# Experts of a two-layer mixture: quarter-row gathers, 32x32 block transposes, and another spread of the products over the quadrants

## The chip, the cores and the metric

One core of a Trainium2 chip runs the whole program. The metric is the device time of one execution in microseconds (us). Short names of the engines: PE is TensorE's matmul side and PEld its weight loads, DVE is VectorE, ACT is ScalarE, POOL is GpSimd and SP is SyncE, which issues most of the DMAs.

## What is computed

The reference is two blocks of two layers each, in float32. The part that matters here is the feed-forward part of the second block, in both of its layers: a hierarchical mixture of experts. Each token (768 of them in the first such layer, 512 in the second) picks two of 32 experts and is sent through both:

```python
def expert_block(args):
    xb, e = args
    return (jax.nn.silu(xb @ w1[e]) * (xb @ w3[e])) @ w2[e]
...
y = yb.reshape(n_rows, d)[dest] * sw[:, None].astype(h.dtype)
return jnp.zeros_like(h).at[stok].add(y)
```

A token has 1024 features, an expert 512 inner ones; w1 and w3 are 1024 x 512, w2 is 512 x 1024. So an expert has 6.29 MB of weights. Two picks of 768 tokens over 32 experts are 48 rows for an expert on average, two of 512 are 32.

## The kernel before, in words

The layers run one after the other: `rwkv`, `mla`, `ab`, the first mixture `m0`, `c`, the second mixture `m1`. Only the two mixtures are touched. `moe` (L2889) lets the router finish (`route`, L2701), then runs `experts` (L2918), then `overflow` (L3056) for what does not fit in the static slots.

**The slots.** Each expert has 96 slots. `route` works out, for slot s of expert e, the token in it: `rd[s, e]` (L2786 to L2789), by one-hot products on PE (L2785), a copy on ACT (L2788) and an addition on DVE (L2789). An empty slot points to a row of zeros on reading and past the end on writing, where the write is dropped.

**One expert, as `experts` has it.** `gather` (L2936) is one indirect DMA issued by POOL: 96 rows of 4 KB from `hbuf` in DRAM to `xg` [96, 1024], with two buffers. `turn` (L2942) makes `xT` [128, 8, 96] of it: eight transposes on PE (L2947), a copy on DVE (L2951) and one on ACT (L2949). The first products take each block of 32 slots as weights (128 x 32, one column quadrant of PE) and stream 512 columns of w1 or w3:

```python
for a in range(3):
    mm(H1[q(a)], lhsT=xT[:, kb, q(a)], rhs=w[0][:, kb, :], **f)
mm(H1[q(3)], lhsT=xT[:, kb, q(2)], rhs=w[1][:, kb, :], **f)
for a in range(2):
    mm(H3[q(a)], lhsT=xT[:, kb, q(a)], rhs=w[1][:, kb, :], **f)
```

(L3021 to L3025.) So of the six products of each of eight `kb`, quadrants 0 and 1 have two each, quadrants 2 and 3 one each. `act` (L2954) makes u of them: tanh on ACT (L2957), three operations on DVE (L2958 to L2960). `uturn` (L2963) transposes u on PE (L2966), with a copy on ACT (L2968). The second products are `yab` (L3008 to L3011: 16 products, eight each in quadrants 2 and 3) and `yc` (L3013 to L3015: eight products, four each in quadrants 0 and 1). `gate` (L2971) makes weight times gate, on ACT (L2974, L2977) and POOL (L2978, in the first mixture only). `yput` (L2981) multiplies by it on DVE (L2985, L2986), and POOL issues an indirect DMA (L2987) that adds the rows to `acc` (`out` in the second mixture) in DRAM.

**The loop.** Step e (L2999) has the first products of expert e and the second products of expert e - 1, mixed. The order of the instructions within the engines is not that of the code: a scheduler with a simulated time line sets it, except inside `manual_schedule`, where the engines named keep the order of the code. Before the change, `experts` has none.

**The weights.** They come in thirds of 2 MB (w1, w3, w2 of one expert) to seven places in turn (`load`, L1498, the DMA on L1503), nearly all issued by SP. A third is issued when the place's earlier content has been used: w3 of expert e takes the place of w1 of expert e - 2, w2 of e that of w3 of e - 2, w1 of e that of w2 of e - 3.

**The start.** The router's last products for the overflow (`pto`, L2883) and for the slots' weights (L2849) come in steps 1 and 0 of the loop, when the generator `own.way` is sent on.

Of the kernel before, what the change touches and what calls it, by code (L numbers as in the profile page):

```python
# [16 lines left out]
P = 128  # L17
# [14 lines left out]
# ---------------------------------------------------------------- host layout  # L32
# [11 lines left out]
def const_arrays(np):  # L44
    """Masks, identities and rope tables: they depend on shapes alone."""
# [43 lines left out]
    put("tid", np.arange(6)[None, :] * P + i[:, None])  # L89
    off["base"] = (base, 0)  # L90
# [28 lines left out]
    # by pairs of heads: queries (64 plain features, 32 to rotate, those with their halves swapped), keys, values, gate  # L119
# [12 lines left out]
    # by units: a key, its four queries, its value  # L132
# [18 lines left out]
# ---------------------------------------------------------------- program  # L151
# [4 lines left out]
def rsqrt(g, v, n, name, pool=None):  # L156
    """v [128, n] -> v ** -0.5, by Newton steps from the exponent's half."""
# [36 lines left out]
def stats(g, tiles, name, junk):  # L194
    """rsqrt(mean(t * t) + eps) of each [128, 1024] tile: [128, n]."""
# [9 lines left out]
def hT_make(g, psum, pool, tiles, A, B, put, name):  # L205
    """tiles: token tiles of one stream; (x rstd) transposed, times A[:, fb] plus B[:, fb], into put(fb)."""
# [16 lines left out]
def affine(g, pool, gcol, MC, sc0, sh0, v, name):  # L223
    """norm gain times (1 + scale), and shift, as [128, 8] columns."""
# [8 lines left out]
def row_bcast(g, psum, MC, g0, v, dst, tag="mm"):  # L233
    """Column block MC[:, g0 : g0 + 8, v] as a row on every partition: dst [128, 1024]."""
# [10 lines left out]
def setup(g):  # L245
# [12 lines left out]
    # silu of the four conditioning vectors, one column of 32 each  # L258
# [10 lines left out]
def rwkv_layer(g):  # L269
# [8 lines left out]
    with contextlib.ExitStack() as own, tc.tile_pool(name="rwB", bufs=1) as keep:  # L278
        # tanh(xw @ w1) and xa @ a1, feature-major; the former with a row of ones for w0
# [62 lines left out]
def rwkv_lerp(g, s, j, affine=False):  # L342
    """The j-th interpolation of the rows; those that are projected by blocks also go to DRAM, by token tiles."""
# [5 lines left out]
    for fb in range(9):  # L349
# [9 lines left out]
        for (A, B, hB), o, n in zip(s.affine, (1, 259), (256, 512)) if affine and fb < 8 else ():  # L359
            # the first and the last row of a stream have one neighbour only  # L360
# [8 lines left out]
def rwkv_first(g, s, L, wap, dst):  # L369
    """Products of a lerp with 128 columns; yields between them."""  # L370
# [21 lines left out]
def mm(g, out, **kw):  # L392
    """A product; how much of the array it keeps busy goes into g.act, and its time in ns into g.ns."""
# [9 lines left out]
def apart(g, later, *earlier):  # L403
    """Accesses to different quadrants of a PSUM bank: no order between them."""
# [4 lines left out]
class Stream:  # L409
    """Parts of work in order; each part is due some time after the one before it, or what that one yields."""  # L410
# [18 lines left out]
class Mix:  # L429
    """Puts streams into one order for the array: what is due and has got the least far. In between, the large  # L430
# [2487 lines left out]
def experts(g, l, own, rd, wi):  # L2918
# [5 lines left out]
    with tc.tile_pool(name="exT", bufs=2, reuse_waits="tile") as pt, \  # L2924
# [74 lines left out]
        for e in range(NE + 1):  # L2999
# [18 lines left out]
            for kb in range(8):  # L3018
# [7 lines left out]
                if e and kb == 1:  # L3026
                    uT = uturn(u)
# [213 lines left out]
```

## Time and profile before

| What | us |
|---|---|
| median of 3 runs | 4262.28 |
| lowest and highest of them | 4259.32, 4266.27 |
| the profiled execution: its span, first to last instruction | 4260.4 |
| PE busy in it | 3810.4 |
| DVE, ACT, POOL busy in it | 2104.5, 1334.9, 735.4 |

The profile is one execution of the program. The page gives no other time of that execution than its span, 1.9 us below the median of the runs; what lies around the span is not shown. A float32 product of 512 columns shows as two records on PE, each with a weight load of its own. "x8" is a count of records, "mean ns" the mean duration of one, and what follows "<-" is what ended an engine's idle time. DMA shares are of the core's 16 DMA engines.

### The profile page before, as it was taken

The page shows a single profiled execution, that of the slowest core. Times are in us where ns is not written, and L with a number is a line of the kernel's source. Part 1 is how long each engine was busy: PE and PEld are TensorE (multiplying, and loading weights), DVE is VectorE, ACT ScalarE, POOL GpSimd, SP SyncE. Part 2 cuts the span into 40 slices and gives each one's busy share as a digit, 9 for nine tenths or more (in the row PEclk, how much of TensorE's full clock was granted, in tenths as well). Part 3 has the DMA queues.
Part 4 walks back from the last instruction along what each step waited for, and adds up shares of the span by engine and source line. Part 5 has one row for each costly group of instructions (what it writes and reads, how often), then busy time and mean ns, then how long its engine had stood idle before and what let it go on. Part 6 is the DMA issues. An engine that isn't in the chain of part 4 may idle for free. (4 is left out here: it accounts for less than half of the span.)

```text
span 4260.4 us, 85407 instructions
## 1 busy us (share of the span) xinstructions
PE 3810.4 (89%) x35570; PEld 2419.0 (57%) x35570; DVE 2104.5 (49%) x5178; ACT 1334.9 (31%) x3262; POOL 735.4 (17%) x668
## 2 busy tenths in 40 slices
PE   6798999999868899987998799999788996999998
PEld 4677777777754667656765333333378863333332
DVE  7435545455543566568765422222376754222222
ACT  3244334434422354333442112112245531111111
POOL 1111001101100111122112222222233312111110
PEclk9899999999977999988999899999889998999999
DMA  6755566666672110210111689899511126888885
GB/s 225 211 173 175 173 185 200 186 201 206 187 209 58 65 55 29 70 41 23 44 51 71 228 323 348 341 346 349 205 40 49 40 69 243 318 334 341 344 336 191
DMA packets 396625, 775.21 MB, mean 182 GB/s; under 512 B 60172, under 2 KB 312012, under 8 KB 370636
## 3 DMA queue, kind: packets, MB, share of 16 engines
q1 hardware_dynamic: 372024, 704.56, 47.1%
q0 software_dynamic: 17504, 56.66, 4.6%
q10 hardware_dynamic: 6708, 8.49, 0.6%
q8 instruction: 282, 4.62, 0.4%
q14 instruction: 107, 0.88, 0.1%
HBM read 711.90 MB, written 66.62 MB: 183 GB/s over the span
## 5 line engine op out<-in xcount | busy, mean ns | idle before, releaser
L3022 PE MATMUL H<-wex,xT 128*32 128x512 f32 x3072 | 772.7, 600 | 0.1
L3025 PE MATMUL H<-wex,xT 128*32 128x512 f32 x2048 | 546.2, 593 | 0.0
L3011 PE MATMUL Y<-wex,uT 128*32 128x512 f32 x2048 | 534.9, 594 | 1.8 <-ACTq L3064 1.8
L3023 PE MATMUL H<-wex,xT 128*32 128x512 f32 x1024 | 521.0, 603 | 0.0
L2951 DVE COPY xT<-pxT 128x384 f32<-128x384 f32 x64 | 35.7, 558 | 598.4 <-PE pxT L2947 595.9
L3025 PEld LDWEIGHTS H<-wex,xT 128*32 128x32 f32 x2048 | 124.2, 110 | 301.8 <-issue 301.5
L3022 PEld LDWEIGHTS H<-wex,xT 128*32 128x32 f32 x3072 | 160.2, 109 | 232.9 <-issue 221.0
L400 PE MATMUL pd<-dw,dl 128*128 128x128 f32 x1536 | 241.7, 301 | 34.1 <-DMA dl<-Ld 25.0
L3015 PE MATMUL Y<-wex,uT 128*32 128x512 f32 x1024 | 236.8, 593 | 0.0
L400 PEld LDWEIGHTS pd<-dw,dl 128*128 128x128 f32 x1536 | 203.2, 204 | 53.2 <-DMA dl<-Ld 25.4
L400 PE MATMUL pd<-dl,dw 128*128 128x128 f32 x1344 | 218.5, 300 | 8.4 <-ACT rk L521 4.6
L1202 ACT ACTIVATE prob<-S,smx 128x768 f32<-128x768 f32 (+3 forms) x160 | 125.7, 786 | 238.2 <-DVE smx L1197 214.0
L2974 ACT ACTIVATE R<-R,wi 96x1024 f32<-96x1024 f32 x64 | 73.4, 1148 | 395.4 <-DVE yo L2986 391.9
L400 PEld LDWEIGHTS pd<-dl,dw 128*128 128x128 f32 x1344 | 178.5, 201 | 27.6 <-issue 10.6
L2485 PE MATMUL pu<-wc,hT 128*128 128x384 f32 (+1 forms) x768 | 184.1, 328 | 1.0 <-ACT hT L1350 1.0
L1140 DVE COPY RT<-ZU 32x128 f32<-32x128 f32 x192 | 54.4, 284 | 255.3 <-PE ZU L400 225.3
L2949 ACT COPY xT<-pxT 128x384 f32<-128x384 f32 x64 | 30.7, 479 | 444.9 <-PE pxT L2947 444.9
L2958 DVE SCALAR_TENSOR_TENSOR th<-th,H 96x512 f32<-96x512 f32 x64 | 43.7, 683 | 244.0 <-ACT th L2957 244.0
L1195 DVE TENSOR_REDUCE smx<-S 128x1 f32<-128x768 f32 (+3 forms) x160 | 128.6, 804 | 67.6 <-PE S L1873 37.7
L3011 PEld LDWEIGHTS Y<-wex,uT 128*32 128x32 f32 x2048 | 132.7, 110 | 49.2 <-issue 46.9
L3015 PEld LDWEIGHTS Y<-wex,uT 128*32 128x32 f32 x1024 | 60.5, 110 | 148.3 <-issue 148.3
L1226 PE MATMUL ppT<-cst,prob 128*128 128x128 f32 x784 | 121.7, 287 | 24.7 <-DVE prob L2291 14.6
(594 smaller groups left out, 8345.7 us busy)
## 6 DMA issues: line engine op xcount, KB each, us to landing
wex<-in_w SPq DMA_DIRECT2D x186, 2048.0 KB, 12.6
dl<-Ld SPq DMA_DIRECT2D x180, 512.0 KB, 3.9
wmod<-in_mod_w SPq DMA_DIRECT2D x128, 512.0 KB, 5.2
dw<-in_rw_in SPq DMA_DIRECT2D x30, 512.0 KB, 5.5
wex<-in_w POOLq DMA_DIRECT2D x6, 2048.0 KB, 9.8
wcr<-in_c_in SPq DMA_DIRECT2D x28, 384.0 KB, 4.0
Ld<-lerp SPq DMA_DIRECT2D x18, 512.0 KB, 6.5
lerp<-in_mod_w SPq DMA_DIRECT2D x4, 2048.0 KB
```

What stands on the lines that cost most here:

```text
L400: return g.nc.tensor.matmul(out, **kw)
L1140: ev = f(dst, Up[u])
L1195: nc.vector.tensor_reduce(m[:, 0:1], S[:, :n], mybir.AxisListType.X, ALU.max)
L1202: nc.scalar.activation(p[:, :n], S[:, :n], AF.Exp, scale=scale, bias=m[:, 1:2], accum_out=m[:, 2:3])
L1226: nc.tensor.transpose(pp[:, k, :], p[:, (i + k) * P:(i + k + 1) * P], g.C("ident"))
L2485: nc.tensor.matmul(o, lhsT=x, rhs=w[:, a:3, kb, :], start=kb == i == 0, stop=kb == 7 and i == 2)
L2974: nc.scalar.activation(G_, Gb[0][0:S], AF.Copy, scale=wi[:, 0, e:e + 1])
L3011: mm(Y[h][q(2 + a)], lhsT=uT[:, fb, q(a)], rhs=w2[:, fb, 512 * h:512 * h + 512], start=fb == 0, stop=fb == 3)
L3015: mm(Y[h][q(h)], lhsT=uT[:, fb, q(2)], rhs=w2[:, fb, 512 * h:512 * h + 512], start=fb == 0, stop=fb == 3)
L3022: mm(H1[q(a)], lhsT=xT[:, kb, q(a)], rhs=w[0][:, kb, :], **f)
L3023: mm(H1[q(3)], lhsT=xT[:, kb, q(2)], rhs=w[1][:, kb, :], **f)
L3025: mm(H3[q(a)], lhsT=xT[:, kb, q(a)], rhs=w[1][:, kb, :], **f)
```

## The change

`gather` becomes three indirect DMAs. The DRAM rows are seen as quarter rows of 256 features, and DMA a brings block a of 32 slots to all 128 partitions: partition 32 q + j gets quarter q of slot j. `route` works out the indices of the quarter rows, `rq` [128, 3, 32]. `turn` is one instruction on DVE that transposes 32x32 blocks, straight to `xT` [128, 3, 8, 32] in SBUF. The quadrants of the products depend on the expert's parity (`hb`, 0 or 2), the second products of the last block of slots (`c`) are split in two halves, one at the end of the step and one in the first two `kb` of the next, and they have a PSUM tile of their own (`Yc`). `experts` runs with PE in the order of the code. `th` and the operations on L2957 and L2958 have 128 partitions instead of 96. The comments and docstrings that the change also drops are left out of the diff here.

```diff
@@ const_arrays
     put("tid", np.arange(6)[None, :] * P + i[:, None])
+    put("row4", i // 32)
@@ route
+    first4 = sc([1], "first4")
+    V.tensor_scalar(first4, g.C("row4"), 4.0 * ntk, None, ALU.add)
+    quad = sc([3, 4, 32], "quad", BF16)
+    V.tensor_copy(quad, g.C("ident")[:, 0:SLOTS].rearrange("p (a j) -> p a j", a=3).unsqueeze(2).to_broadcast([P, 3, 4, 32]))
...
         nc.tensor.matmul(pt_[0:SLOTS], lhsT=oh[:, i], rhs=vv[:, i], start=i == 0, stop=i == K - 1)
+    two = sc([2, 32], "two", BF16)
+    V.tensor_copy(two[0:SLOTS], pt_[0:SLOTS])
+    rq = own.rq = keep.tile([P, 3, 32], U32, name="rq")
+    pq = ps.tile([P, 3, 2, 32], F32, name="pq", tag="aux")
+    for a in range(3):
+        nc.tensor.matmul(pq[:, a], lhsT=quad[0:SLOTS, a].rearrange("p g j -> p (g j)"), rhs=two[0:SLOTS], start=True, stop=True)
+    part4 = sc([3, 32], "part4")
+    nc.scalar.activation(part4, pq[:, :, 1], AF.Identity, scale=4.0, bias=first4)
+    V.scalar_tensor_tensor(rq, pq[:, :, 0], 4.0, part4, ALU.mult, ALU.add)
@@ moe
-        experts(g, l, into, rd, wi)
+        with tc.manual_schedule(engines=PEO):
+            experts(g, l, into, rd, wi)
@@ experts
+    quarters = hbuf[:, :].rearrange("n (q f) -> (n q) f", q=4)
...
-            tc.tile_pool(name="psX", bufs=2, space=PSUM) as psx:
+            tc.tile_pool(name="psX", bufs=1, space=PSUM) as psx:
...
         def gather(e):
-            xg = pt.tile([S, D], F32, name="xg", tag="xg")
-            own.gather = nc.gpsimd.indirect_dma_start(out=xg, out_offset=None, in_=hbuf[:, :],
-                                         in_offset=bass.IndirectOffsetOnAxis(ap=rd[:, e:e + 1], axis=0))
+            xg = pt.tile([P, 3, 256], F32, name="xg", tag="xg")
+            for a in range(3):
+                own.gather = nc.gpsimd.indirect_dma_start(out=xg[:, a], out_offset=None, in_=quarters,
+                                                          in_offset=bass.IndirectOffsetOnAxis(ap=own.rq[:, a, e:e + 1], axis=0))
             return xg

         def turn(xg):
-            xT = pt.tile([P, 8, S], F32, name="xT", tag="xT")
-            for h in range(2):
-                p = psx.tile([P, 4, S], F32, name="pxT", tag="tr")
-                for k in range(4):
-                    nc.tensor.transpose(p[:, k, :], xg[:, 4 * h + k::8], ident[0:S, 0:S])
-                if h:
-                    nc.scalar.copy(xT[:, 4:8, :], p)
-                else:
-                    nc.vector.tensor_copy(xT[:, 0:4, :], p)
+            xT = pt.tile([P, 3, 8, 32], F32, name="xT", tag="xT")
+            nc.vector.transpose(xT.rearrange("p a k t -> p (a k) t"), xg.rearrange("p a (i k) -> p a k i", k=8))
             return xT
...
+        class Second:
+            def __init__(self, e, u, w2, hb):
+                self.e, self.u, self.w2, self.hb, self.lb = e, u, w2, hb, 2 - hb
+                self.i = 0
+            def start(self):
+                self.uT = uturn(self.u)
+                self.Y = [psy.tile([P, 512], F32, name="Y%d" % h, tag="Y%d" % h) for h in range(2)]
+            def ab(self):
+                h, fb = self.i // 4, self.i % 4
+                self.i += 1
+                for a in range(2):
+                    mm(self.Y[h][q(self.lb + a)], lhsT=self.uT[:, fb, q(a)], rhs=self.w2[:, fb, 512 * h:512 * h + 512], start=fb == 0, stop=fb == 3)
+            def c(self, fb):
+                if fb == 0:
+                    self.Yc = psy.tile([P, 512], F32, name="Yc", tag="Yc")
+                for h in range(2):
+                    mm(self.Yc[q(self.hb + h)], lhsT=self.uT[:, fb, q(2)], rhs=self.w2[:, fb, 512 * h:512 * h + 512], start=fb == 0, stop=fb == 3)
...
             for kb in range(8):
                 if cur:
                     f = dict(start=kb == 0, stop=kb == 7)
-                    for a in range(3):
-                        mm(H1[q(a)], lhsT=xT[:, kb, q(a)], rhs=w[0][:, kb, :], **f)
-                    mm(H1[q(3)], lhsT=xT[:, kb, q(2)], rhs=w[1][:, kb, :], **f)
+                    for a, to in ((0, hb), (1, hb + 1), (2, lb)):
+                        mm(H1[q(to)], lhsT=xT[:, a, kb, :], rhs=w[0][:, kb, :], **f)
+                    mm(H1[q(lb + 1)], lhsT=xT[:, 2, kb, :], rhs=w[1][:, kb, :], **f)
                     for a in range(2):
-                        mm(H3[q(a)], lhsT=xT[:, kb, q(a)], rhs=w[1][:, kb, :], **f)
-                if e and kb == 1:
-                    uT = uturn(u)
-                if e and kb >= 2:
-                    yab(i)
-                    i += 1
+                        mm(H3[q(hb + a)], lhsT=xT[:, a, kb, :], rhs=w[1][:, kb, :], **f)
+                if old and kb < 2:
+                    old.c(2 + kb)
+                    if kb == 1:
+                        old.put_c()
+                if y and kb == 1:
+                    y.start()
+                if y and kb >= 2:
+                    y.ab()
                 if kb == 5 and e + 1 < NE:
                     xTn = turn(xg)
...
-            if e:
-                G_ = gate(e - 1)
-            if e:
-                for k in range(4):
-                    if i < 8:
-                        yab(i)
-                        i += 1
-                    yc(k)
-                yput(Y, e - 1)
+            if y:
+                for k in range(2):
+                    y.ab()
+                    y.c(k)
+                y.put_ab()
+            old = y
             if cur:
-                prev = (act(H1, H3), w[2])
+                y = Second(e, act(H1, H3, hb), w[2], 2 - hb)
...
+        for k in (2, 3):
+            old.c(k)
+        old.put_c()
```

Here `hb = 2 * (e % 2)` and `lb = 2 - hb` are set at the top of a step. `put_ab` and `put_c` are the two halves of the former `yput`: the first two blocks of slots, with `gate`, and the last block with the adding DMA.

## Rows read from the trace of the kernel before

**Rows 1.** Page, part 1: busy us (share), records of each engine.

```profile
PE 3810.4 (89%) x35570; PEld 2419.0 (57%) x35570; DVE 2104.5 (49%) x5178; ACT 1334.9 (31%) x3262; POOL 735.4 (17%) x668
```

**Rows 2.** A stretch of 21 us: length, busy (PE, PEld, DVE, ACT, POOL), clock, DMA share, GB/s.

```profile
2474.00:2495.00 21.00, 21.00 (x166) 7.37 (x160) 5.51 (x9) 3.85 (x5) 4.79 (x3) 1.00 0.95 365
```

**Rows 3.** PE in order of time over one step: start us, length us, instruction.

```profile
2717.12 0.72 PE L2966 MATMUL puT<-cst,u 96*128 96x96 f32 x4
2717.77 0.63 PE L3022 MATMUL H<-wex,xT 128*32 128x512 f32 x3
...
2725.68 1.13 PE L2947 MATMUL pxT<-cst,xg 96*128 96x96 f32 x8
...
2731.49 0.60 PE L3015 MATMUL Y<-wex,uT 128*32 128x512 f32 x2
...
2731.92 1.89 PE L3015 MATMUL Y<-wex,uT 128*32 128x512 f32 x8
...
2737.19 0.72 PE L2966 MATMUL puT<-cst,u 96*128 96x96 f32 x4
```

**Rows 4.** DMA queues over one step, 2717.8 to 2737.87 us.

```profile
DMA packets 658, 7.00 MB, mean 349 GB/s; under 512 B 108, under 2 KB 108, under 8 KB 272
```

**Rows 5.** DMA queues, 2692.5 to 2699.5 us: packets, MB, share of 16 engines.

```profile
q1 hardware_dynamic: 198, 2.98, 99.9%
```

**Rows 6.** DMA queues, 2861.5 to 2867.5 us, an adding DMA beside the weights.

```profile
q1 hardware_dynamic: 110, 1.69, 67.2%
q0 software_dynamic: 97, 0.38, 31.4%
```

**Rows 7.** DMA queues, 2728.5 to 2730 us, a gather with no weights under way.

```profile
q0 software_dynamic: 76, 0.31, 76.4%
```

**Rows 8.** DMA queues, 3250 to 3260 us, another stage: packets of 1 KB.

```profile
q1 hardware_dynamic: 1438, 1.42, 51.5%
```

**Rows 9.** DMA issues, whole span: count, median us to landing; adding DMAs of both mixtures.

```profile
acc<-yo,rd POOLq DMA_INDIRECT x32, 11.4
...
out<-yo,rd POOLq DMA_INDIRECT x32, 11.2
```

**Rows 10.** All engines, 2708.8 to 2709.9 us: end of an expert's w1, next issue.

```profile
2708.88 0.59 PE L3023 MATMUL H<-wex,xT 128*32 128x512 f32 x1
...
2709.52 0.33 SPq L1503 DMA_DIRECT2D wex<-in_w  x1
```

**Rows 11.** Groups by line, whole span: block transposes on DVE, POOL's work.

```profile
L2978 POOL TENSOR_TENSOR R<-R,R 96x1024 f32<-96x1024 f32 x32 | 90.3, 2823 | 8.5 <-ACT R L2977 8.5
...
L2938 POOL DMA_INDIRECT xg<-hbuf,rd x64 | 59.5, 930 | 477.6 <-PE pxT L2947 474.7 <-DVE nb L2823 1.6 <-DVE blk L2866 0.7
...
L1004 DVE STREAM_TRANSPOSE F<-AB 128x512 f32<-128x512 f32 x16 | 16.1, 1042 | 5.1 <-ACT AB L993 5.0
```

**Rows 12.** In order of time, start of the first mixture: turn, first product.

```profile
2402.77 1.54 PE L2947 MATMUL pxT<-cst,xg 96*128 96x96 f32 x8 [6.10 <-DMA xg<-hbuf,rd]
...
2406.09 1.07 PE L3022 MATMUL H<-wex,xT 128*32 128x512 f32 x3
```

**Rows 13.** PE in order of time: step 1's start and last `uturn` of each mixture.

```profile
2423.30 0.63 PE L3022 MATMUL H<-wex,xT 128*32 128x512 f32 x3
...
2443.71 0.87 PE L2883 MATMUL pto<-bv,oho 128*128 128x48 f32 x6
...
3053.43 0.72 PE L2966 MATMUL puT<-cst,u 96*128 96x96 f32 x4
...
3609.05 0.63 PE L3022 MATMUL H<-wex,xT 128*32 128x512 f32 x3
...
4235.78 0.72 PE L2966 MATMUL puT<-cst,u 96*128 96x96 f32 x4
```

**Rows 14.** DVE and ACT in order of time: `act` of one expert.

```profile
2709.57 0.59 ACT L2957 ACTIVATE th<-H 96x512 f32<-96x512 f32 x1 [2.29 <-PE H L3023]
...
2711.68 0.69 DVE L2960 SCALAR_TENSOR_TENSOR u<-th,H 32x512 f32<-32x512 f32 x1
```

More of the change, by code (lines that the diff above doesn't have):

```diff
@@ L2936, in gather, with act @@
         def gather(e):
-            xg = pt.tile([S, D], F32, name="xg", tag="xg")
-            own.gather = nc.gpsimd.indirect_dma_start(out=xg, out_offset=None, in_=hbuf[:, :],
-                                         in_offset=bass.IndirectOffsetOnAxis(ap=rd[:, e:e + 1], axis=0))
+            xg = pt.tile([P, 3, 256], F32, name="xg", tag="xg")
+            for a in range(3):
+                own.gather = nc.gpsimd.indirect_dma_start(out=xg[:, a], out_offset=None, in_=quarters,
+                                                          in_offset=bass.IndirectOffsetOnAxis(ap=own.rq[:, a, e:e + 1], axis=0))
             return xg
         def turn(xg):
-            xT = pt.tile([P, 8, S], F32, name="xT", tag="xT")
-            for h in range(2):
-                p = psx.tile([P, 4, S], F32, name="pxT", tag="tr")
-                for k in range(4):
-                    nc.tensor.transpose(p[:, k, :], xg[:, 4 * h + k::8], ident[0:S, 0:S])
-                if h:
-                    nc.scalar.copy(xT[:, 4:8, :], p)
-                else:
-                    nc.vector.tensor_copy(xT[:, 0:4, :], p)
-            return xT
-        def act(H1, H3):
-            th = new("th", [S, 512], 1)
+            xT = pt.tile([P, 3, 8, 32], F32, name="xT", tag="xT")
+            nc.vector.transpose(xT.rearrange("p a k t -> p (a k) t"), xg.rearrange("p a (i k) -> p a k i", k=8))
+            return xT
+        def act(H1, H3, hb):
+            lb = 2 - hb
+            th = new("th", [P, 512], 1)
             u = new("u", [S, 512])
-            nc.scalar.activation(th, H1[0:S], AF.Tanh, scale=0.5)
-            nc.vector.scalar_tensor_tensor(th, th, 1.0, H1[0:S], ALU.add, ALU.mult)
-            nc.vector.scalar_tensor_tensor(u[0:64], th[0:64], 0.5, H3[0:64], ALU.mult, ALU.mult)
-            nc.vector.scalar_tensor_tensor(u[64:96], th[64:96], 0.5, H1[96:128], ALU.mult, ALU.mult)
+            nc.scalar.activation(th, H1, AF.Tanh, scale=0.5)
+            nc.vector.scalar_tensor_tensor(th, th, 1.0, H1, ALU.add, ALU.mult)
+            nc.vector.scalar_tensor_tensor(u[0:64], th[q(hb, 2)], 0.5, H3[q(hb, 2)], ALU.mult, ALU.mult)
+            nc.vector.scalar_tensor_tensor(u[64:96], th[q(lb)], 0.5, H1[q(lb + 1)], ALU.mult, ALU.mult)
             return u
@@ L2979, in gate @@
             return G_
-        def yput(Y, e):
-            yo = new("yo", [S, D])
-            for h in range(2):
-                cs = slice(512 * h, 512 * h + 512)
-                nc.vector.tensor_tensor(out=yo[0:64, cs], in0=G_[0:64, cs], in1=Y[h][64:128], op=ALU.mult)
-                nc.vector.tensor_tensor(out=yo[64:96, cs], in0=G_[64:96, cs], in1=Y[h][32 * h:32 * h + 32], op=ALU.mult)
-            nc.gpsimd.indirect_dma_start(out=acc[:, :], out_offset=bass.IndirectOffsetOnAxis(ap=rd[:, e:e + 1], axis=0),
-                                         in_=yo, in_offset=None, bounds_check=own.nt * P - 1, oob_is_err=False, compute_op=ALU.add)
@@ L2990, in experts, with put_ab, put_c @@
-        mm = nc.tensor.matmul
+        mm = nc.tensor.matmul
+        class Second:
[15 more added lines that the diff above has]
+                    mm(self.Yc[q(self.hb + h)], lhsT=self.uT[:, fb, q(2)], rhs=self.w2[:, fb, 512 * h:512 * h + 512], start=fb == 0, stop=fb == 3)
+            def put_ab(self):
+                self.G = gate(self.e)
+                self.yo = new("yo", [S, D])
+                for h in range(2):
+                    cs = slice(512 * h, 512 * h + 512)
+                    nc.vector.tensor_tensor(out=self.yo[0:64, cs], in0=self.G[0:64, cs], in1=self.Y[h][q(self.lb, 2)], op=ALU.mult)
+            def put_c(self):
+                for h in range(2):
+                    cs = slice(512 * h, 512 * h + 512)
+                    nc.vector.tensor_tensor(out=self.yo[64:96, cs], in0=self.G[64:96, cs], in1=self.Yc[q(self.hb + h)], op=ALU.mult)
+                nc.gpsimd.indirect_dma_start(out=acc[:, :], out_offset=bass.IndirectOffsetOnAxis(ap=rd[:, self.e:self.e + 1], axis=0),
+                                             in_=self.yo, in_offset=None, bounds_check=own.nt * P - 1, oob_is_err=False, compute_op=ALU.add)
@@ L2997, in experts @@
         w = own.weights(0)
-        prev = None
+        y = old = None
         for e in range(NE + 1):
             cur = e < NE
+            hb = 2 * (e % 2)
+            lb = 2 - hb
             if cur:
@@ L3003, in experts @@
                 H3 = psh.tile([P, 512], F32, name="H3", tag="H3")
-            if e:
-                u, w2 = prev
-                Y = [psy.tile([P, 512], F32, name="Y%d" % h, tag="Y%d" % h) for h in range(2)]
-            def yab(i):
-                h, fb = i // 4, i % 4
-                for a in range(2):
-                    mm(Y[h][q(2 + a)], lhsT=uT[:, fb, q(a)], rhs=w2[:, fb, 512 * h:512 * h + 512], start=fb == 0, stop=fb == 3)
-            def yc(fb):
-                for h in range(2):
-                    mm(Y[h][q(h)], lhsT=uT[:, fb, q(2)], rhs=w2[:, fb, 512 * h:512 * h + 512], start=fb == 0, stop=fb == 3)
-            i = 0
             for kb in range(8):
```

3 lines of the change are left out of this document (1 added, 2 removed).

## The prediction

> **What bounds the kernel now.** The page comes first: PE is busy for 89% of the span, far ahead of DVE with 49% [rows 1]. Then stretches of 21 us through both mixtures: PE is busy for the whole stretch, at a granted clock of 1.00, while the DMA engines are busy for up to 0.95 of it [rows 2]. So PE sets the step of one expert, but the transfers are close behind it. Third, PE in order of time over one step [rows 3]: from `uturn` to `uturn` it takes 2737.19 - 2717.12 = 20.07 us. Inside, a round of records follows the last after 0.43 us (2731.49 to 2731.92), up to four quadrants in a round; a product is two records, so 0.86 us of its quadrant. Quadrants 0 and 1 have 16 + 4 = 20 products in a step, quadrants 2 and 3 have 16. The fullest quadrant therefore needs 20 x 0.86 = 17.2 us; `uturn` takes 0.65 (2717.12 to 2717.77) and `turn` 1.13. That is 19.0, and 1.1 us more go to rounds that are not full: the last row but one shows eight records of the last block, two quadrants at a time.
>
> **PE after the change.** By the code, the fuller pair of quadrants in a step has 16 first products and 2 of `c`, the other pair 8 first products, 8 of `ab` and 2 of the older `c`: 18 each, written in rounds of four. 18 x 0.86 = 15.5, plus 0.65 for `uturn`; `turn` is gone. I add 0.25 for emptying the array round `uturn`, between 0 and the 1.1 lost now: 16.4 us, between 16.15 and 17.25.
>
> **The transfers after it.** They then decide, so a step's DMA time has to be added up. Per step 7.00 MB move now [rows 4], 6.29 of them weights. Alone, the weights keep the engines 99.9% busy at 2.98 MB in 7 us, 426 GB/s [rows 5]: 14.8 us for an expert. The adding DMA: beside one of 0.38 MB, some 92 rows, the weights moved 1.69 MB in 6 us instead of 2.56 [rows 6], a loss of 0.87 MB or 2.0 us. Ordinary experts have 48 rows in the first mixture and 32 in the second, yet these DMAs land after 11.4 and 11.2 us [rows 9], so I take 2.0 for all: 96 slots over 16 engines are six to an engine, and the engine that has six full ones is as late with few rows as with many. By bytes it would be 0.2 MB, 0.5 us, the lower end. The Trainium skill (DMA: Bandwidth & Descriptors, Queues, rings and completion order) has each DMA engine take turns between its queues, a packet at a time; the two equal landings agree. By that rule a step comes to the sum below, by bytes alone to 1.5 us less.
>
> The gather now has 384 packets of 1 KB in place of 96 of 4 KB, the same bytes. The trace of before has no indirect packets of 1 KB. Plain ones took 0.515 x 16 x 10 us / 1438 = 57 ns each [rows 8]; indirect ones of 4 KB 0.764 x 16 x 1.5 us / 76 = 241 ns [rows 7]. I take 57, as a packet's time goes with its bytes in all these rows (16 KB of weights take 615 ns: 16 x 7 us over 2.98 MB / 16 KB): 384 x 57 / 16 engines = 1.4 us. By bytes at 426 GB/s it would be 0.9, at 241 ns it would be 5.8.
>
> Sum: 14.8 + 2.0 + 1.4 = 18.2 us a step, 1.8 above PE's 16.4. At the lower ends it is 16.2 and PE's 16.4 rules; at the upper it is 22.6. Can the queue be kept full? SP issues the third that takes w1's place 0.05 us after its last record (2708.88 + 0.59 = 2709.47, issue at 2709.52) [rows 10]. In the new order that issue stands some 2.6 us (three rounds of products) ahead of the next expert's start, so the next batch begins as the last of the earlier one lands. w1, whose place is now used until the second `kb` of the next step, 3.4 us in, is issued later than before, but w3 and w2 stand ahead of it on SP with 2 x 4.9 us to move; that costs nothing as long as they do.
>
> **Other engines.** DVE: a block transpose of 512 columns took 1042 ns [rows 11], so 768 take 1.56, in place of a copy of some 0.56; with 5.5 us busy in 21 now [rows 2] it has room, and xT is needed only two `kb` later. ACT loses a copy. POOL issues three gathers of 0.93 instead of one and has 2.82 for the gates in the first mixture [rows 11]: with the adding DMA about 7 us of 18. A gather may start when `turn` has freed its buffer, two steps before it is needed, so even a landing of 16 us (24 packets an engine, each behind one of weights at 615 + 57 ns) is covered. `act` ends 2712.37 - 2709.57 = 2.8 us after tanh starts [rows 14]; the new `uturn` comes 1.7 (tail) + 3.4 (two `kb`) = 5.1 us after the first products. Should DVE do `put_ab` first, PE could wait for about 0.6 us, hidden while the transfers leave it 1.8 idle.
>
> **Start and end of a mixture.** `route` gains a copy, three small products, and indices that pass ACT and DVE as before: 1.1 us by its neighbours, all ahead of the gather. The third gather is issued 2 x 0.93 = 1.9 later. `turn` before, from its first record to the first product, took 2406.09 - 2402.77 = 3.3 us [rows 12]; the block transpose with its wait some 1.8. Together +1.5 a mixture (0 to 4). Step 1 has `pto` of the overflow in PE's order: 6 records take 0.87 [rows 13], 24 take 3.5, and I allow 0.7 for waits on its one-hots (0 to 3): 15.5 + 0.65 + 4.2 = 20.35, say 20.5. The last expert's products run half empty as now, 10 rounds instead of about 9.3: +0.6.
>
> **Sum.** From step 1 to the last `uturn`, 31 steps, the mixtures now take 3053.43 - 2423.30 = 630.1 and 4235.78 - 3609.05 = 626.7 us [rows 13]. After: 20.5 + 30 x 18.2 = 566.5 each. Gains 63.6 + 60.2 = 123.8, less 2 x 1.5 and 2 x 0.6: 119.6. From the span of 4260.4 that gives 4140.8; the median of the runs stands 1.9 above that span, so 4143.
>
> **Rivals.**
> A: the transfers overlap better than I add them up, and PE's 16.4 rules. 60 steps x 1.8 less: 4035. For it: the lower ends. Against: 14.8 is weights alone at 99.9% busy.
> B: the chip gives no more over whole steps than it gives now. The best stretch of 21 us moved 365 GB/s [rows 2]; 7.00 MB at that rate are 19.2 us, 60 x 1.0 more: 4203. For it: no long stretch is above that. Against: the 426 of 7 us, and PE now leaves pauses between batches.
> The Trainium skill (DMA: Bandwidth & Descriptors, Where 436 GB/s comes from) puts the limit of HBM for a core at about 358 GB/s, which speaks against this change: 19.6 us a step by it. The 426 GB/s measured over 7 us do not agree.
> C, the slower one: the quarter rows cost by the packet. At 241 ns the gather takes 5.8 us of the engines, a step 22.6, 60 x 4.4 more than forecast: 4407. It decides from a step of 20.2, where the 119.6 are used up: (20.2 - 16.8) x 16 / 384 = 142 ns a packet. For it: the only indirect packets measured take 241. Against: their bytes.
> D: the even spread is not achieved, PE needs as many rounds as now and only `turn` is saved: 20.07 - 1.13 = 18.9 a step, 60 x 0.7 more: 4185. Against: the new order goes round the quadrants without a break.
>
> **How the numbers follow.** Forecast 0.56, A 0.10, B 0.16, C 0.09, D 0.09. The range leaves out A and C: 4080 (steps of 17.2, the adding DMA at half its price) to 4215 (19.4, a gather packet at 107 ns). Faster is all but C, 0.91; C may stop near its deciding point, so slower 0.07 and the same 0.02. Within 0.2%, 8.5 us, is about what a measurement of this kernel can't tell from no change.
>
> **What would show it.** Right: `uturn` to `uturn` at 17.8 to 18.6 us, PE waiting for `wex` before a step's first product, rounds of four without gaps, DMA share near 1.0. Wrong: steps of 16.4 without waits (A); DMA share near 1.0 with 1 KB packets far above 57 ns (C); DMA share well below 1.0 and PE waiting for u, xT or a late issue, a step on which I have put no price.

## The result, and the profile after

The kernel after takes 4142.12 us (median of 4 runs, 4135.81 to 4143.87), the kernel before in the same series 4262.54 (4259.32 to 4266.27). The ratio is 0.9711, with a 95% interval from 0.9697 to 0.9725: 2.9% faster. The profiled execution of after has a span of 4141.0 us, 119.4 less than that of before; forecast were 119.6. The number is close, but the way to it is not quite the one I wrote down.

Part 1 of the page of after, to be held against [rows 1]:

```profile
PE 3610.6 (87%) x35064; PEld 2310.0 (56%) x35064; DVE 2163.4 (52%) x5186; ACT 1305.2 (32%) x3200; POOL 863.5 (21%) x796
```

PE has 200 us less work, DVE and POOL have more. But only 119 us of the 200 came off the time: PE now waits. For what, the groups by line of the page say (busy, mean ns | idle before them, and what ended it):

```profile
L3056 PE MATMUL H<-wex,xT 128*32 128x512 f32 x3072 | 568.5, 612 | 68.0 <-DMA wex<-in_w 51.6
L3057 PE MATMUL H<-wex,xT 128*32 128x512 f32 x1024 | 542.6, 613 | 15.1 <-DMA wex<-in_w 15.1
...
L2958 POOL DMA_INDIRECT xg<-hbuf,rq x192 | 184.4, 960 | 531.8 <-DVE xT L2965 446.8
...
L2965 DVE STREAM_TRANSPOSE xT<-xg 128x768 f32<-128x768 f32 x64 | 102.3, 1598 | 83.1 <-PE H L3059 79.2
```

L3056 and L3057 are the first products with w1 and with w3. They waited 51.6 and 15.1 us for weights (`wex`). The block transpose takes 1.60 us (1.56 forecast), a gather's issue 0.96 (0.93).

Now the steps. PE in order of time in after, the `uturn` of five steps in a row, in the columns of [rows 3]:

```profile
2523.94 0.60 PE L2982 MATMUL puT<-cst,u 96*128 96x96 f32 x3
2540.17 0.60 PE L2982 MATMUL puT<-cst,u 96*128 96x96 f32 x3
2556.64 0.60 PE L2982 MATMUL puT<-cst,u 96*128 96x96 f32 x3
2582.50 0.60 PE L2982 MATMUL puT<-cst,u 96*128 96x96 f32 x3
2598.74 0.60 PE L2982 MATMUL puT<-cst,u 96*128 96x96 f32 x3
```

The steps are 16.23, 16.47, 25.86 and 16.24 us. So PE keeps its own pace of 16.24 us (16.4 forecast) in most steps, and every seventh step is 6.6 to 10 us longer; of the others some are longer by up to 5.4 us, in most sevens two. Read in this way through both mixtures, the mean of the 31 steps is 18.25 us in the first and 18.15 in the second, against the forecast 18.2. Step 1 (long, with `pto` in it) and the last step (short, 14.5 us) are in that mean. The long ones come every seven steps, in both mixtures at the same experts: 25.86, 26.29, 25.13, 22.86 in the first and 26.27, 25.73, 25.44, 24.04 in the second. Step 1 of each takes 24.6 and 25.1.

One long step from nearby, all engines in order of time, 2568 to 2578 us, with what ended the idle time in brackets:

```profile
2568.28 1.58 DVE L2965 STREAM_TRANSPOSE xT<-xg 128x768 f32<-128x768 f32 x1
...
2568.91 0.60 PE L3021 MATMUL Yc<-wex,uT 128*32 128x512 f32 x2
...
2576.99 1.07 PE L3056 MATMUL H<-wex,xT 128*32 128x512 f32 x3 [7.47 <-DMA wex<-in_w]
...
2577.85 1.07 PE L3056 MATMUL H<-wex,xT 128*32 128x512 f32 x3
```

xT has been there since 2569.86; the first product of expert 9 waits 7.47 us for its w1. Then its records take 1.07 us where they took 0.60: PE, after having stood still, works at the lower of its two clock levels (1.2 GHz) for some rounds: from 2577 to 2580 us the granted clock is 0.50, from 2583 us on it is 1.00 again. The view of three longer stretches (length, busy PE, PEld, DVE, ACT, POOL, granted clock, DMA share, GB/s) shows it, against [rows 2]:

```profile
2542.00:2556.00 14.00, 14.00 (x135) 4.96 (x128) 4.91 (x6) 2.63 (x3) 6.00 (x5) 1.00 1.02 415
2574.00:2598.00 24.00, 21.01 (x176) 6.47 (x180) 6.26 (x8) 3.37 (x4) 5.84 (x4) 0.86 0.79 301
2705.00:2725.00 20.00, 19.39 (x156) 5.90 (x160) 4.38 (x6) 3.37 (x4) 3.91 (x2) 0.86 0.82 298
```

In the undisturbed steps the transfers run at 415 GB/s with the engines fully busy. After a long wait the clock is 0.86 and the DMA share falls to 0.79: PE stood still and released no place, and SP issued nothing from 2567.83 to 2582.64 us. The DMA queues over 400 us, 2500 to 2900 (packets, MB, share of 16 engines), against [rows 4]:

```profile
DMA packets 14978, 150.31 MB, mean 376 GB/s; under 512 B 3408, under 2 KB 3408, under 8 KB 6600
...
q1 hardware_dynamic: 9393, 136.76, 84.0%
q0 software_dynamic: 5554, 13.09, 12.1%
```

q1 has the weights: 136.76 MB are 21.74 experts of 6.29 MB. The two queues were busy for 96.1% of 400 us, so 384.4 / 21.74 = 17.7 us of DMA time a step. The table below gives this figure for the other kernels, always from the same 400 us. In these 400 us the engines idle for the other 3.9%, 0.7 us a step.

Start and end, to be held against [rows 12] and [rows 13] (PE and DVE in order of time):

```profile
2409.04 1.55 DVE L2965 STREAM_TRANSPOSE xT<-xg 128x768 f32<-128x768 f32 x1 [1.05 <-DMA xg<-hbuf,rq]
...
2410.85 1.07 PE L3056 MATMUL H<-wex,xT 128*32 128x512 f32 x3 [8.33 <-DVE xT L2965]
...
2426.76 0.63 PE L3056 MATMUL H<-wex,xT 128*32 128x512 f32 x3
...
2996.12 0.73 PE L2982 MATMUL puT<-cst,u 96*128 96x96 f32 x4
...
3551.57 0.63 PE L3056 MATMUL H<-wex,xT 128*32 128x512 f32 x3
...
4117.83 0.72 PE L2982 MATMUL puT<-cst,u 96*128 96x96 f32 x4
```

From step 1 to the last `uturn` the mixtures take 569.4 and 566.3 us (forecast 566.5 each); 60.8 and 60.5 us are gained there, and 1.8 of these 121.2 are lost at the starts and ends (4.2 forecast).

**Which load is late.** The trace names all thirds `wex`. The compiled program has them in SP's order, here for the experts 8 to 11 (an expert's three tiles have neighbouring numbers, w1 the lowest):

```
907 L1504 DMA wex_25065<-in_w1     908 wex_25067<-in_w3     909 wex_25069<-in_w2
910 L1504 DMA wex_25180<-in_w3     911 wex_25182<-in_w2     912 wex_25178<-in_w1
913 L1504 DMA wex_25293<-in_w3     914 wex_25295<-in_w2     915 wex_25291<-in_w1
916 L1504 DMA wex_25404<-in_w1     917 wex_25408<-in_w2     918 wex_25406<-in_w3
```

The scheduler has moved w1 behind w3 and w2 for the experts 9 and 10, and w3 behind w2 for 11 and 12; the pattern repeats every seven experts, like the code's seven places, three of them in one pool and four in another. But w2 is needed a step after w1. In the trace, the three loads of expert 9 are issued at 2550.52, 2551.36 and 2556.74 us: w1 goes out last, 12.8 us before the end of PE's last record of that step (2568.91 + 0.60), with two loads ahead of it. The steps that are longer by a smaller amount belong to the experts whose w3 goes out last: 21.59 and 16.31 us for the experts 11 and 12, 17.79 and 21.51 for 18 and 19. The second late w1 of a pair costs nothing: that of expert 10 goes out at 2582.64 us, when nothing has been issued for 15 us, and its step takes 16.24.

### The profile page after: what moved, and what is told of

Its sections match the earlier page's. It is cut to its first block, busy times and chain, and to the rows that moved or that the text cites. A ratio compares the mean times of both kernels' runs of the same rounds, so it can differ in the third digit from the quotient of the medians.

```text
span 4141.0 us, 84438 instructions
## 1 busy us (share of the span) xinstructions
PE 3610.6 (87%) x35064; PEld 2310.0 (56%) x35064; DVE 2163.4 (52%) x5186; ACT 1305.2 (32%) x3200; POOL 863.5 (21%) x796
## 5 line engine op out<-in xcount | busy, mean ns | idle before, releaser
L3056 PE MATMUL H<-wex,xT 128*32 128x512 f32 x3072 | 568.5, 612 | 68.0 <-DMA wex<-in_w 51.6
L3057 PE MATMUL H<-wex,xT 128*32 128x512 f32 x1024 | 542.6, 613 | 15.1 <-DMA wex<-in_w 15.1
L3059 PE MATMUL H<-wex,xT 128*32 128x512 f32 x2048 | 537.9, 604 | 0.0
L3015 PE MATMUL Y<-wex,uT 128*32 128x512 f32 x2048 | 506.6, 596 | 1.3 <-ACT uT L2984 1.2
L3056 PEld LDWEIGHTS H<-wex,xT 128*32 128x32 f32 x3072 | 126.8, 112 | 340.1 <-issue 274.8
L3028 DVE TENSOR_TENSOR yo<-R,Y 64x512 f32<-64x512 f32 x128 | 87.6, 685 | 416.7 <-PE Y L3015 228.2
L2958 POOL DMA_INDIRECT xg<-hbuf,rq x192 | 184.4, 960 | 531.8 <-DVE xT L2965 446.8
L3021 PE MATMUL Yc<-wex,uT 128*32 128x512 f32 x1024 | 292.7, 618 | 0.0
L3059 PEld LDWEIGHTS H<-wex,xT 128*32 128x32 f32 x2048 | 120.8, 112 | 241.7 <-issue 235.2
L2984 ACT COPY uT<-puT 128x384 f32<-128x384 f32 x64 | 30.7, 479 | 482.0 <-PE puT L2982 482.0
L3033 DVE TENSOR_TENSOR yo<-R,Yc 32x512 f32<-32x512 f32 x128 | 87.6, 684 | 179.1 <-PE Yc L3021 178.2
L2973 ACT ACTIVATE th<-H 128x512 f32<-128x512 f32 x64 | 38.2, 597 | 400.7 <-PE H L3057 366.8
L2965 DVE STREAM_TRANSPOSE xT<-xg 128x768 f32<-128x768 f32 x64 | 102.3, 1598 | 83.1 <-PE H L3059 79.2
L1227 PE MATMUL ppT<-cst,prob 128*128 128x128 f32 x784 | 122.3, 288 | 26.4 <-DVE prob L2292 16.1
```

Source lines behind the costliest of these rows:

```text
L1227: nc.tensor.transpose(pp[:, k, :], p[:, (i + k) * P:(i + k + 1) * P], g.C("ident"))
L2958: own.gather = nc.gpsimd.indirect_dma_start(out=xg[:, a], out_offset=None, in_=quarters, in_offset=bass.IndirectOffsetOnAxis(ap=own.rq[:, ...
L2965: nc.vector.transpose(xT.rearrange("p a k t -> p (a k) t"), xg.rearrange("p a (i k) -> p a k i", k=8))
L3015: mm(self.Y[h][q(self.lb + a)], lhsT=self.uT[:, fb, q(a)], rhs=self.w2[:, fb, 512 * h:512 * h + 512], start=fb == 0, stop=fb == 3)
L3021: mm(self.Yc[q(self.hb + h)], lhsT=self.uT[:, fb, q(2)], rhs=self.w2[:, fb, 512 * h:512 * h + 512], start=fb == 0, stop=fb == 3)
L3056: mm(H1[q(to)], lhsT=xT[:, a, kb, :], rhs=w[0][:, kb, :], **f)
```

## The experiments

My theory after the result: the transfers set the mean step, and PE's own pace of 16.24 us shows only between the waits. The first rival: PE's work sets the time, so each saved us of it counts. The second: the order of the loads makes the steps long, not their amount. The columns: median us; ratio to the kernel before, with its interval; the mean of all 31 steps in either mixture, from one profiled execution; the pace that most undisturbed steps have; the DMA time a step as above.

| kernel | us | ratio | steps | pace | DMA |
|---|---|---|---|---|---|
| after | 4142.12 | 0.9711 (0.9697 to 0.9725) | 18.25, 18.15 | 16.24 | 17.7 |
| e1_full_rows | 4214.13 | 0.9881 (0.9864 to 0.9897) | 19.42, 19.21 | 17.74 | 18.4 |
| e2_old_quadrants | 4161.55 | 0.9753 (0.9733 to 0.9773) | 18.55, 18.17 | 17.95 | 17.8 |
| e3_less_weights | 4027.30 | 0.9454 (0.9434 to 0.9475) | 16.45, 16.43 | 16.24 | 13.3 |
| e4_load_order | 4095.72 | 0.9610 (0.9588 to 0.9632) | 17.52, 17.47 | 16.24 | 17.4 |
| e5_slots | 4091.90 | 0.9604 (0.9577 to 0.9631) | 17.51, 17.51 | 16.24 | 17.3 |
| e6_slots_order | 4038.65 | 0.9486 (0.9463 to 0.9509) | 16.75, 16.42 | 16.24 | 16.9 |
| e7_full_rows_order | 4176.78 | 0.9804 (0.9781 to 0.9826) | 18.64, 18.57 | 17.74 | 18.4 |
| e8_fixed_order | 4132.04 | 0.9712 (0.9684 to 0.9740) | 17.87, 17.96 | – | 17.3 |
| e9_before_order_slots | 4267.32 | 1.0006 (0.9994 to 1.0019) | 20.10, 20.02 | 20.05 | 18.0 |
| e10_full_rows_order_slots | 4132.48 | 0.9686 (0.9668 to 0.9703) | 18.03, 17.88 | 17.74 | 18.3 |
| e11_order_skip | 4070.61 | 0.9551 (0.9530 to 0.9571) | 17.14, 16.97 | 16.24 | 17.0 |
| e12_all_three | 4030.89 | 0.9452 (0.9437 to 0.9467) | 16.50, 16.42 | 16.24 | 16.6 |

**e1_full_rows: the spread alone.** `gather` and `turn` as before, in the new loop; the two halves of `turn` stand after `kb` 4 and 6, since there is one PSUM buffer for them.

```diff
-                if kb == 5 and e + 1 < NE:
-                    xTn = turn(xg)
+                if kb == 4 and e + 1 < NE:
+                    xTn = turn(xg, 0)
+                if kb == 6 and e + 1 < NE:
+                    turn(xg, 1, xTn)
```

> The gather and the turn of the kernel before (whole rows, eight transposes by TensorE a step, two PSUM copies) under the even spread of the kernel after. TensorE's own step, 16.24 us in the undisturbed steps after, grows by the turn's 1.13 us to about 17.4. If the transfers set the mean step (18.2 us), TensorE's 17.4 stays hidden under them: 4135 to 4165 us, uturn to uturn still 18.0 to 18.5. If TensorE's work sets it, each of 62 steps is 1.13 us longer: about 4212 us.

Measured: 4214.13, near the rival's number, 72 us above after. PE's pace rose by 1.50 us and the mean step by 1.1 to 1.2. The long steps are still there, every seventh. My theory missed here. But the DMA time went up too, to 18.4 us a step, which neither side had foreseen; e7 and e10 look into this.

**e2_old_quadrants: the gather and the transpose alone.** Quarter rows and VectorE's transpose, with `act`, the loop and `yput` of the kernel before (`xT[:, a, kb, :]` for `xT[:, kb, q(a)]`). PE stays in the order of the code, as in after; in the kernel before, the scheduler set it.

> Quarter rows and VectorE's transpose stay, the products go back to the quadrants of the kernel before (20 full-width equivalents and the loss of rounds that are not full). TensorE's own step is then that of the kernel before less its turn, 20.07 - 1.13 = 18.9 us, just over the transfers' 18.2. Theory (two limits, the larger one counts): 18.2 to 18.9 a step, 4142 to 4185 us. If the even spread were worth nothing beside the turn: 4142. If both halves of the change were needed in equal shares and added up (TensorE alone sets the time): half of the 120 us is lost, about 4200.

Measured: 4161.55, inside the theory's span. PE's pace is 17.95 us: the turn, and whatever the scheduler's order of PE added to it, cost the kernel before 20.05 - 17.95 = 2.1 us a step. No run takes these two apart. The spread then takes 17.95 - 16.24 = 1.71 us off the pace, just two products of 0.86, but 19 us off the time: the transfers (17.8) are reached after the first half of the change.

**e3_less_weights: two thirds of the weights.** w3 is not loaded and w1 stands in for it, so this kernel computes something else. The seven places now hold three and a half experts, so the loads also go out earlier.

```diff
-        queue.dma_start(t, self.g.I[("w1", "w3", "w2")[n % 3]][self.l, n // 3]...
+        queue.dma_start(t, self.g.I[("w1", "w2")[n % 2]][self.l, n // 2]...
```

> w3 is not loaded, and w1 takes its place in the products: the same TensorE work with two thirds of the weight transfers (the output is not the reference's). Transfers: 9.9 + 2.0 + 1.4 = 13.3 us a step, below TensorE's 16.24. If transfers set the mean step now, every step becomes 16.2 to 16.4 and the time 4142 - 62 x 1.95 = about 4021 us (4015 to 4035), with no wait for wex in the middle steps and the granted clock at 1.00 there. If waits for u, uT or xT are behind the long steps, they stay and the time is over 4080.

Measured: 4027.30. Apart from step 1 and the short last one, nearly every step is 16.24 us (one is 16.34), with no wait for `wex` from 2500 to 2960 us, and the DMA time is 13.3 us as worked out. So the long steps of after are waits for weights and nothing else. One stretch of 200 us in this kernel (columns as above):

```profile
2600.00:2800.00 200.00, 200.00 (x1828) 64.37 (x1824) 76.64 (x98) 41.07 (x49) 81.34 (x60) 1.00 0.84 295
```

**e4_load_order: the same bytes in another order.** w1 and w3 of expert e + 1 ahead of w2 of e, with seven places as before, and each SP load tied behind the last one, so that the scheduler can't swap them.

```diff
+        self.plan = sorted(..., key=lambda x: 3 * x[0] + (-1, 0, 4)[x[1]] if x[0] > 0 else (-3, -2, 4)[x[1]])
...
-        queue.dma_start(t, ...)
+        e, m = self.plan[n]
+        with self.g.tc.issue_after(behind.ins) if behind else contextlib.nullcontext():
+            x = queue.dma_start(t, ...)
...
-        while len(self.w) < 3 * e + 3:
+        while len(self.w) < min(3 * e + 5, 3 * NE):
```

> The same transfers in another order: w1 and w3 of the next expert ahead of w2 of this one, fixed on SP's queue, so that each load has 18 to 29 us of lead, where w1 had 12.5 in the kernel after. If the sum of the transfers sets the mean step, only the DMA engines' idle time can go (mean busy share 0.971 in 2500 to 2960): 18.2 x 0.97 = 17.7 us a step, about 31 us, 4111 (4100 to 4130). If it is the order (w1 behind a w2 that is needed a step later, in two steps of seven), the steps come down to 16.3 to 16.6 and the time to about 4030 to 4045. If nothing hangs on the order: 4142.

Measured: 4095.72, 46 us less than after, a little beyond the lower end for "sum of the transfers" (4100) and far from the 4030 to 4045 of the order alone. The long steps are gone: seven steps at 16.24 after step 1, then 16.3 to 19.3 us without a pattern, with the DMA engines busy throughout. In this run, from 2500 to 2900 us:

```profile
q1 hardware_dynamic: 9915, 144.40, 87.1%
q0 software_dynamic: 5802, 13.69, 12.5%
```

That is 99.6%. Both causes are real: the new plan of the loads gains 46 us (what of it is the order and what the tie, e8 shows below), and with the DMA engines full the transfers hold the step above 16.24. Where PE now waits is worth seeing, since it hardly shows as idle time (PE of e4_load_order in order of time):

```profile
2742.42 0.63 PE L3021 MATMUL Y<-wex,uT 128*32 128x512 f32 x2
2742.80 1.10 PE L3062 MATMUL H<-wex,xT 128*32 128x512 f32 x5
2744.11 0.62 PE L3063 MATMUL H<-wex,xT 128*32 128x512 f32 x1 [0.20 <-DMA wex<-in_w]
```

Five records stand in 1.31 us, from 2742.80 to 2744.11, where three rounds of four would. The products with w1 go on in their quadrants, the one with w3 (L3063) waits for its load; the array is half empty, and the page counts PE as busy. PE's weight loads show the wait; 2600 to 2900 us, total us, times, longest:

```profile
PEld H L3063 <- DMA wex<-in_w: 16.0, 17, 1.5
```

That is once in every step, 0.9 us each.

**e5_slots: where the full slots lie.** Nothing but the slot that a token gets: rank r goes to slot 6 (r mod 16) + r div 16.

```diff
-        V.tensor_tensor(out=oh[:, k * nt:(k + 1) * nt], in0=row(g.C("io128")[:, 0:SLOTS], SLOTS), ...
+        V.tensor_tensor(out=oh[:, k * nt:(k + 1) * nt].rearrange("p t (b a) -> p t b a", a=6),
+                        in0=g.C("io128")[:, 0:SLOTS].rearrange("p (a b) -> p b a", b=16)..., ...
```

> The loads in the order of the kernel after, but an expert's tokens are put into slots 0, 6, 12, ... (rank r in slot 6 (r mod 16) + r div 16), so that, if the adding DMA's 96 slots lie six to an engine in order, its rows are spread over all 16 engines instead of filling six slots on a few. Theory (the engine with six full slots sets when a load has landed, 0.33 us a full slot): with 48 and 32 tokens an expert some three and two full slots on each engine in place of six on some, 0.8 to 1.1 us less a step on the slowest engine, landings closer to the end of the count of packets (now 1 to 5 us behind), shorter long steps: 4095 to 4125 us. If the mean over the engines counts, or the slots do not lie so: 4142.

Measured: 4091.90, 50 us less than after, 0.8 us a step, a little more than expected. The bytes are the same. The long steps have shrunk from 25.86, 26.29, 25.13 to 20.73, 22.78, 23.00. This is what the term "the engine that has six full slots is late" asks for. The Trainium skill (DMA: Bandwidth & Descriptors, Why a DMA increments its semaphore by 16 and not by 1) says that a DMA has landed only when the last of its engines has finished its share; these runs fit that. The adding DMA of one expert with 49 rows, the third from last of the first mixture's, runs with nothing beside it. Its queue and its landing in after (2983.4 to 2988.8 us), then in e5_slots (2961.9 to 2966.1 us):

```profile
q0 software_dynamic: 112, 0.20, 26.4%
acc<-yo,rd POOLq DMA_INDIRECT x1, 5.4
...
q0 software_dynamic: 112, 0.20, 35.9%
acc<-yo,rd POOLq DMA_INDIRECT x1, 4.2
```

The same packets and bytes land 1.2 us sooner. The traces hold each packet's start: in after, 9 packets of 4 KB start within 0.1 us, the rest as these end; in e5_slots, 16 start within 0.2 us. 49 rows at six to an engine need 9 engines, so the slots do lie six neighbours to an engine.

**e6_slots_order: both.** The edits of e4_load_order and e5_slots.

> Both: the load order of e4_load_order and the spread slots. e4_load_order ran at TensorE's 16.24 for eight steps, then at 17.5 to 18.2, with the DMA engines 0.989 busy: the transfers. If the slowest engine sets that rate, it falls by 0.8 to 1.1 us to 16.7 to 17.0 in 23 steps of each mixture: 4096 - 45 = about 4050 us (4035 to 4065). If the mean over the engines sets it, nothing changes: 4096.

Measured: 4038.65, as the theory of the slowest engine has it. The second mixture runs at PE's 16.24 in every step after step 1, the first one in the fifteen steps after step 1; the fourteen after them take 16.3 to 18.0.

**e7_full_rows_order and e10_full_rows_order_slots: why e1 missed.** e1_full_rows with the load order of e4_load_order, then with the slots too.

> e1_full_rows (TensorE's step 17.74) with the load order of e4_load_order. If e1_full_rows lost its 72 us because the late w1 comes on top of whatever TensorE does, then with the order mended the transfers' 17.8 hide TensorE's 17.74: only the first eight steps of each mixture are longer, by 1.5 us, so 4096 + 24 = about 4120 us (4105 to 4135). If the turn on TensorE costs its time in any case: 4096 + 62 x 1.2 to 1.5 = 4170 to 4190.

> e7_full_rows_order (whole rows, turn on TensorE, new load order; 18.9 us a step where e4_load_order has 17.8, DMA engines 0.991 busy) with the spread slots. If its 1.1 us above e4_load_order is the same crowding of engines (the engines with full slots have their gathered rows and their added rows both), spreading takes it away and TensorE's 17.74 is left: 4039 + 60 x 1.50 = 4129 us (4115 to 4140). If whole rows cost the DMA engines more than quarter rows in themselves, 1.1 us stays on the transfers: over 18.0 a step, 4150 to 4170.

Measured: 4176.78 for the first, in the span of "the turn costs its time in any case", but not for that reason: after seven or eight steps at PE's 17.74 its steps are 18 to 20 us, with the DMA engines full. Its queues from 2500 to 2900 us, to be held against those of e4_load_order above:

```profile
q1 hardware_dynamic: 9268, 134.99, 86.3%
q0 software_dynamic: 4729, 12.70, 12.5%
```

98.8% busy, but 21.46 experts where e4_load_order moved 22.95: 18.4 us of DMA time a step against 17.4. So with whole rows and the turn on PE a step takes 1.06 us more of the DMA engines than with quarter rows and the turn on DVE, for the same bytes. Most of it stands in the weights' own queue: 86.3% of 400 us over 21.46 experts are 16.1 us, against 15.2 in e4_load_order; the indirect DMAs have 2.3 against 2.2. With the slots spread, 4132.48 (4129 expected): nearly every step is PE's 17.74, and the turn costs its 1.5 us. In e1_full_rows, then, both are at work: its undisturbed steps run at PE's 17.74, and its DMA time is 18.4 us a step with the engines 5% idle. How its 72 us divide between them is not shown. Whether the rows or the turn lengthen the DMA time, and why, is open too.

**e8_fixed_order: only the swap undone.** Places and program order as in after, SP's loads tied in that order.

> The places and the program order of the kernel after, only that SP may not swap the loads: w1, w3, w2 of each expert one behind the other. If it is the swap alone (w1 behind w2 in two steps of seven) that makes the long steps, they go and the time is near that of e4_load_order: 4095 to 4115 us. But now w3 and w2 wait on SP behind a w1 whose place comes free late, so that w3 has 12.5 us of lead and no longer 18. If leads this short count, every step waits for w1 or w3, 18.0 to 18.5 us evenly: 4135 to 4165.

Measured: 4132.04, just below the span of the second case. The pattern of sevens is gone, but most steps are now 16.6 to 18.8 us, and PE waits for w3 (L3061) in 18 of some 26. Waits of PE in that run, 2500 to 2960 us (total us, times, longest):

```profile
PE H L3061 <- DMA wex<-in_w: 15.8, 18, 2.7
```

and in after, for the same stretch:

```profile
PE H L3056 <- DMA wex<-in_w: 20.7, 3, 7.5
PE H L3057 <- DMA wex<-in_w: 7.9, 6, 2.7
```

So the swap makes the pattern of sevens, but undoing it alone gains nothing clear of the noise: 10 us by the medians, while the ratios to before are 0.9712 and 0.9711. The gain of e4_load_order comes with its other plan: longer leads for w1 and w3, a shorter one for w2.

**e9_before_order_slots: the same two edits without the change.**

> The kernel before with the load order of e4_load_order and the slots of e5_slots, nothing of the change. If TensorE's 20.07 us bounded the step before and the transfers lay under it, nothing moves: 4255 to 4265 us, and the change is then worth 4262 - 4039 = 223 us where the transfers are out of its way, against 120 without. If late loads cost the kernel before as well, up to 40 us of it goes: 4220 to 4250.

Measured: 4267.32, ratio 1.0006: no difference. The kernel before was bound by PE (20.05 us, with 18.0 of DMA time under it), as the prediction read it. With both edits the change is worth 1.0006 - 0.9486 = 5.2% of the time, some 222 us, where it brought 2.9% by itself.

**e11_order_skip and e12_all_three: no rows for empty slots.** The gather gets a bound and drops the indices beyond it, from the third expert on.

```diff
+                          **(dict(bounds_check=4 * P * own.nt - 1, oob_is_err=False) if e > 1 else {}))
```

> e4_load_order, but from the third expert on the gather reads no row for an empty slot (half of 96 slots in the mixture over 768 tokens, two thirds in that over 512; what lies in their places is never added up). By the prediction's price, 1.4 us for 96 rows spread over 16 engines, 0.7 and 0.9 us less a step in the 23 steps of each mixture that wait for transfers: 4096 - 37 = about 4059 us. If what counts is the engine with full slots, which saves little: 4085 to 4100.

> Load order, spread slots and no rows for empty slots together. e6_slots_order still has 8 us of steps above 16.24 in its first mixture and none in its second; with less to transfer they go: 4039 - 8 = 4031 us (4022 to 4040). If something else than transfers makes those steps long: 4039.

Measured: 4070.61 for e11, 25 us less than e4_load_order: 0.54 us in each of 46 steps, two thirds of the price expected. And 4030.89 for e12 with all three edits: every step after step 1 but the short last one is 16.24 us in both mixtures, no wait for weights shows from 2500 to 2960 us, and the time is within 4 us of the kernel that loads a third less. It leaves nothing out and is the fastest of all that do not, 2.7% below after (4030.89 / 4142.12). Its stretch of 200 us:

```profile
2600.00:2800.00 200.00, 200.00 (x1824) 64.67 (x1820) 78.52 (x102) 40.97 (x49) 84.43 (x63) 1.00 1.01 411
```

In this stretch PE is never idle, at full clock, and the transfers run at 411 GB/s with the engines at 1.01: both limits are reached at once.

## Why the prediction was right, and where not

**What bounds before** held: e9 gives the kernel before the edits that are worth 103 us behind the change, and gains nothing.

**PE's step**: 16.4 forecast, 16.24 measured (e3, e12). Its parts were mis-sized, though: I gave the turn 1.13 us and put 1.1 down to rounds that were not full. e2 shows that without the turn the old spread runs at 17.95, that is 17.2 + 0.65 and 0.1. The loss went with the turn or with the scheduler's order of PE, which e2 drops together: 2.1 us. In the new order the turn alone costs 1.5 (e10 against e6). Rival D, 18.9 us with only the turn saved, was e2; it gave 4161.55 and not 4185, for this reason.

**The transfers' sum**: 18.2 us forecast, 17.7 measured as DMA time in after. Two terms were mis-sized: the weights take 84.0% of 400 us over 21.74 steps, 15.5 us (14.8 forecast, from a stretch with nothing beside them), the indirect DMAs 12.1%, 2.2 us (3.4). The mean step came out at 18.2 because the engines also idled 3 to 4%. So the number was met by luck, by two errors that cancel: half a us too much in the sum, and half a us of waits that I had priced at nothing.

**The step that failed** is "w1 ... is issued later than before, but w3 and w2 stand ahead of it on SP with 2 x 4.9 us to move; that costs nothing as long as they do". The queue does stay nearly full, but full of the wrong load: w1 is what PE needs first, and it has 12.8 us of lead, behind a load that is needed a step later. e4, with the same bytes, is 46 us faster. Program order alone does not mend it (e8): w1 still goes out as late, and PE then waits for the w3 behind it. The sign of this step in the trace was the one that I listed (PE waiting for `wex` before a step's first product); that the steps would be even at 17.8 to 18.6 was wrong: few are.

**The adding DMA**: the mechanism (the engine with six full slots) was right by e5 and e6, which move no byte less and gain 50 and, on top of e4, 57 us, and by the packets shown at e5.

**The gather**: wrong in form. There are no packets of 1 KB. In the queues of after "under 2 KB" is no more than "under 512 B", and 6600 - 3408 = 3192 packets between 2 and 8 KB in 21.74 steps are 147 a step: 96 for the gather and some 50 for the adding DMA, all of 4 KB. So rival C had no ground. Its price, 1.4 us, was an upper value: e11 gets back 0.54 for a half to two thirds of it, so 0.8 to 1.1 for all by estimate. That a step with quarter rows would take less of the DMA engines than one with whole rows and the turn on PE (e7 against e4) was not in the prediction at all. At 1.06 us in each of 62 steps it is worth up to 66 us where the transfers decide, a gain that the sum had at nothing.

**Rivals A and B**: A's time, 4035, is reached as soon as the transfers are out of the way (e3, e6, e12). B is refuted: 365 GB/s was no limit, after moves 415 over 14 us and e12 411 over 200. The Trainium skill's 358 GB/s for a core (DMA: Bandwidth & Descriptors, Where 436 GB/s comes from) does not agree with these stretches either.

**Start**: the transpose to the first product took 1.8 us as forecast. Step 1 takes 24.6 and 24.1 us from first product to first product, some 4 more than I gave it; the thirty steps after it take 544.7 and 542.2 us in place of 546. Here too errors cancel.

## What to carry to other kernels

Here two limits lie within 10% of each other (16.24 and 17.7 us a step), and the time is more than the larger one: the waits of the one on the other come on top. In such a case look at the order in which loads leave the issuing engine (a scheduler may have swapped them), and give what is needed first the longest lead. Once a change has run into the second limit, that limit's small terms count: the order, full rows spread over the DMA engines and empty rows not read gave 111 us more on top of the change's 120 (e12). Two edits that move nothing in the kernel before (e9) are worth 103 us behind the change (e6).

## What was not expected of the hardware

Indirect quarter rows of 1 KB showed as packets of 4 KB, and a step with them had 17.4 us of DMA time, weights included, where one with whole rows of the same bytes and the turn on PE had 18.4 (e4, e7). Rows moved to other slots, with no byte less, gained 50 us (e5): six neighbouring slots of an adding DMA lie on one engine. PE's wait can hide in half-empty rounds: in 200 us of e4_load_order PE counts as busy for 198, while its steps are 1.3 us longer than its pace on average. And a wait of 7.5 us costs 9.6, since the records after it take 1.07 us in place of 0.60.
